# One combine moved behind a gate and up product, and a small projection split around a branch, in the expert layers of a two-block transformer kernel

## The chip, the cores and the metric

The kernel runs on one NeuronCore of a Trainium2 chip. The core has a matrix engine (PE in the profile, with its weight loads as PEld), a vector engine (DVE), a scalar engine (ACT), a general engine (POOL) and a sync engine (SP), whose queue here issues nearly all weight transfers. The engines run side by side, each through its own list of instructions in order, and wait for one another by semaphores. The metric is the device time of one execution in microseconds (us). Three executions of the kernel before took 853.91, 855.52 and 860.98 us.

## The reference, cut to what matters

The whole is an attention block with a dense feed-forward part, followed by two layers that each have attention, a mixture of 32 experts and a gated add of a per-layer input `p`. The change lies in the last two parts of each of the two layers:

```python
for i in range(DEPTH_2):                       # 2 layers
    ...
    h = h + hier_moe(rms_norm_2(h, ln_ffn[i]), ...)
    gate = jax.nn.sigmoid(rms_norm_2(h, ln_ple[i]) @ ple_w_gate[i])
    h = h + (gate * (p[i] @ ple_w_proj[i])).astype(h.dtype)

def hier_moe(xn, ...):                         # 256 tokens, 2 of 32 experts each
    hid = jax.nn.silu(jnp.einsum('td,edf->tef', xt, w_gate)) * jnp.einsum('td,edf->tef', xt, w_up)
    y = jnp.einsum('tef,efd->td', hid * cw[:, :, None], w_down)
```

`p[i]` is 256 x 256 and `ple_w_proj[i]` is 256 x 1024. The product of the two depends on neither the experts nor `h`, so it may stand anywhere ahead of the gated add.

## The kernel before, in words

`moe(l, router, rs)` computes the experts of layer `l` in eight passes `q` of four experts. The experts' weights are streamed once: each pass takes six panels of 1 MB from a stream `W`, four "gate_up" panels (one expert each, two transfers of 512 KB) and two "down" panels (two experts each). The stream's order is that of the generator `experts(l)`. A panel is issued on SP as soon as one of 21 buffers (the arena, tiles `a`) is free and the stream's limit allows it; the transfers use eight completion counters in rotation, so that an issue also waits for the transfer eight places before it.

A pass is this on PE. `gate_up` makes 64 small matmuls into one bank `gu` (line 1025). `hidden` turns the result on ACT and DVE into the hidden values `hd` (lines 1032 to 1034). `turn` transposes them on PE (`ht`, line 1038) and ACT copies the transpose (line 1039). `down` makes 16 matmuls (line 1045) into `y0` and `y1`, each of which ACT rounds (line 1049) and DVE takes the remainder of (line 1050). `combine` adds these to the accumulators `acc` of all tokens with eight matmuls (line 1056). The combine of a pass stands behind the *next* pass's `gate_up`, so PE has work while ACT and DVE make the hidden values. `gather` (line 993) and `slots` (lines 1009 to 1017, tile `ex`) prepare the rows and places of coming passes.

Pass 6 differs, since it is followed by `over.all`: a branch that reruns the chain of a pass for one expert that has more than 32 tokens (tiles `ov`, lines 1104 to 1147). In this input layer 0 takes the branch once and layer 1 does not. Ahead of pass 6's `gate_up` the kernel before makes the combine of pass 5 and the whole of `p @ ple_w_proj`: `ple_T` transposes `p` (four matmuls, tile `tps`, then ACT line 811 and DVE line 812), and `ple_proj` makes 24 matmuls in two halves of columns (tile `pj`, lines 543 to 545). Each half uses two pieces of the weight panel "ple_p", and each piece is first split by `split`: ACT (or POOL) casts it to a high part (line 538 or 536) and DVE (or POOL) subtracts for the low part (line 539). PE and SP keep the order in which the program is written; on ACT, DVE and POOL a scheduler orders the work when the program is built.

The `split` results, the gathered rows `xe` and the rounded `yd` share a ring of five buffers `s`; matmul results share eight PSUM banks, four of which the accumulators hold.

Of the kernel before, what the change touches and what calls it, by code (L numbers as in the profile page):

```python
# [203 lines left out]
class Stream:  # L204
# [24 lines left out]
    def next(self, key):  # L229
        if not self.ready:  # L230
            self.emit()
        k, name, views = self.ready.pop(0)
        assert k == key, (k, key)
        self.pump()
        return name, views
# [16 lines left out]
def block_kernel(ctx, tc, I, out):  # L252
# [14 lines left out]
    def bank(name="bank"):  # L267
        return psum.tile([128, 512], F32, tag="bank", name=name)
# [20 lines left out]
    def kpn(ap):  # L289
        return ap.rearrange("(k p) n -> p k n", p=128)  # L290
# [17 lines left out]

    def experts(l):
        for q in range(8):  # L310
            if q == 6:
                yield from panel("ple_p", kpn(I["ple_w_proj_2"][l]), 2)

            for i in range(4):
                ne, e, k0 = (1, 4 * q + i, 0) if q else (4, 0, 256 * i)

                def load(v, ne=ne, e=e, k0=k0):
                    v = v.rearrange("p (e a n) -> p e a n", e=ne, a=2)
                    for a, src in enumerate((I["moe_w_gate_2"], I["moe_w_up_2"])):
                        nc.sync.dma_start(v[:, :, a], src[l, e:e + ne].rearrange("e (p k) f -> p e (k f)", k=8)  # L320
                                          [:, :, k0:k0 + 1024 // ne])
                    return v

                yield "gate_up", 2048, load
            for e in range(4 * q, 4 * q + 4, 2):
                def load(v, e=e):
                    v = v.rearrange("p (e n) -> p e n", e=2)
                    nc.sync.dma_start(v, I["moe_w_down_2"][l, e:e + 2].rearrange("e p n -> p e n"))
                    return v

                yield "down", 2048, load
        for c in range(2):
            yield from panel("ple_g", kpn(I["ple_w_gate_2"][l])[:, :, c * 512:(c + 1) * 512], 4)
# [91 lines left out]
    def drain(g):  # L425
        for _ in g:
            pass
# [378 lines left out]
    def ple_T(pv_):  # L806
        pT = take("pT", [2, 2, S], F32R)
        b = bank("tps")
        transp2(lambda t, f: pv_[:, t, f * 128:(f + 1) * 128], 0, 2, b)
        hv, lv = [pT[:, i].rearrange("p a s -> p (a s)") for i in range(2)]  # L810
        A.copy(hv, b)
        V.tensor_tensor(lv, b, hv.bitcast(F32), OP.subtract)
        return [pT[:, 0], pT[:, 1]]

    def ple_proj(pT):
        pj = take("pj", [2, 1024])
        name, ws = W.next("ple_p")
        for c in range(2):
            ps = [bank("pj") for _ in range(2)]
            for k in range(2):  # L820
                acc_k(pT, k, ws[k][:, c * 512:(c + 1) * 512], ps, k == 0, k == 1)
                yield
            for t in range(2):
                A.copy(pj[:, t, c * 512:(c + 1) * 512], ps[t])
        W.drop(name)
        drop("pT")
        pjs.append(pj)
# [38 lines left out]
    def moe(l, router, rs):  # L866
# [185 lines left out]
        def combine(T, last):  # L1052
            for c in range(2):
                for hl in range(2):
                    for t in range(2):
                        mm(acc[t][c], T.d[:, t], T.yd[c][:, hl],  # L1056
                           start=False, stop=last and hl == 1)
                if last:
                    with tc.high_priority():
                        for t in range(2):  # L1060
                            (A.copy if t else V.tensor_copy)(h[:, t, c * 512:(c + 1) * 512], acc[t][c])

        class Overflow:
# [75 lines left out]
            def all(self, T, n):  # L1139
                R = Step(new_d(128), T)  # L1140
                self.pick(R.d)
                combine(T, False)
                R.yd = [R.ydt() for _ in range(2)]
                with tc.If(n > 0):
                    self.run(R)
                    with tc.If(n > 1):  # L1146
                        with tc.For_i(1, n, 1):
                            self.find()
                            self.load()
                            self.pick(R.d)  # L1150
                            self.run(R)
                drop("ovg", "ovd", "ovf")

        nrs = Rstd(f"rp{l}")
        prev = None
        for q in range(8):
            names, gu, dn = [], [], []
            if q == 6:
                combine(prev, False)
                prev = None  # L1160
                drain(ple_proj(ple_T(pv_)))
            for i in range(6):
                name, v = W.next("gate_up" if i < 4 else "down")
                names.append(name)
                (gu if i < 4 else dn).append(v)
            if q == 2:
                pv_ = ple_load(l)
            if q == 2:
                W.room(4)
            if q == 3:  # L1170
                over = Overflow()
            if q == 4:
                over.load()
                njob_r = nc.values_load(njob_i[0:1, 0:1], min_val=0, max_val=32)
            if q == 5:
                W.room(6 if l else 9)
            if q == 0:
                g = gather(d, Ts)
                next(g)
                acc_h(1, 1)  # L1180
            T = Ts.pop(0)
            ahead = not Ts and q < 7
            if ahead:
                d, Ts = steps()
            if q == 0:
                for i, _ in enumerate(gate_up(0, T, gu)):
                    if i == 1:
                        drain(g)
                        drain(slots(0, T))
                    W.drop(names.pop(0))  # L1190
            else:
                drain(gate_up(q, T, gu))
            if prev is not None:
                combine(prev, False)
            while len(names) > 2:
                W.drop(names.pop(0))
            fill = chain(gather(d, Ts) if ahead else (), slots(q + 1, Ts[0]) if Ts else ())
            later = rest(0)
            if q == 6:
                fill, later = later, fill  # L1200
            for _ in range(0 if q else 3):
                next(fill, None)
            turn(T)
            for _ in range(9 if q else 1):
                next(fill, None)
            down(T, dn)
            drain(fill)
            drain(later)
            for name in names:
                W.drop(name)  # L1210
            prev = T
            if q == 6:

                over.all(T, njob_r)
                drop("hr0", "hr1")
                prev = None
# [231 lines left out]
    for i, (k, c) in enumerate(jobs):  # L1448
# [4 lines left out]
        if i < 2:  # L1453
            k, c = jobs[i + 2]
# [638 lines left out]
```

## Time and profile before

| | |
|---|---|
| times of three executions | 853.91, 855.52, 860.98 us, median 855.52 |
| the profiled execution | 855.65 us, of which the span in the trace is 853.9 us |
| PE busy | 817.7 us, 96% of the span |
| DVE, ACT, POOL busy | 522.8, 445.1, 226.5 us |
| transfers | 201.71 MB, mean 236 GB/s |
| transfer rate in the later passes of each expert layer | 380 to 410 GB/s |
| mean granted PE clock | 0.994 of full speed |

The page gives busy times, the 40 slices of the span, and the chain of work that ended last. Two things help in reading it. A busy PE row includes matmuls that overlap one another, so the start times of successive groups tell more than their lengths. And a transfer's landing is told as the time from its issue; on SP, an issue that stands later than its neighbours' rhythm shows when an earlier transfer on the same counter landed.

### The profile page before, as it was taken

The numbers are of one execution on the slowest core, as the hardware profiler recorded it, in microseconds if no ns is written. First come the engines' busy times: TensorE is split into PE (matmuls) and PEld (weight loads), VectorE is DVE, ScalarE is ACT, GpSimd is POOL, SyncE is SP. The second block draws the span as 40 slices with busy tenths as digits, with TensorE's granted clock in tenths as the row PEclk, the third lists the DMA queues.
The fourth block names the chain that finished last, engine by engine and source line by source line (L and its number), as shares of the span: only waits on it lengthen the run. The fifth ranks groups of instructions, "written<-read, shape, count | busy, mean of one in ns | idle before, by whom it ended". The sixth has DMA issues, their size and how long they took to land. (4 is left out here: it accounts for less than half of the span.)

```text
span 853.9 us, 15690 instructions
## 1 busy us (share of the span) xinstructions
PE 817.7 (96%) x5660; PEld 639.4 (75%) x5660; DVE 522.8 (61%) x1520; ACT 445.1 (52%) x1085; POOL 226.5 (27%) x293
## 2 busy tenths in 40 slices
PE   8998999999999999999999999988999899999887
PEld 6897878999999988687667666765778577667556
DVE  5778766755455567678875725332888857353354
ACT  5675865644444456457865233332777843333353
POOL 2224542223222222423553400000324434000011
PEclk9999999999999999999999999999999999999999
DMA  9991429655565544173305689999964437899961
GB/s 319 385 376 54 155 74 399 238 178 192 198 197 178 171 152 151 64 244 124 125 1 188 264 333 406 406 409 385 370 221 127 195 106 247 304 405 406 409 245 50
DMA packets 85714, 201.71 MB, mean 236 GB/s; under 512 B 5840, under 2 KB 27776, under 8 KB 85632
## 3 DMA queue, kind: packets, MB, share of 16 engines
q1 hardware_dynamic: 83568, 198.36, 64.1%
q10 hardware_dynamic: 2064, 2.29, 0.9%
q8 instruction: 47, 0.77, 0.4%
q14 instruction: 35, 0.29, 0.1%
HBM read 199.57 MB, written 1.06 MB: 235 GB/s over the span
## 5 line engine op out<-in xcount | busy, mean ns | idle before, releaser
L539 DVE TENSOR_TENSOR s<-a,s 128x512 fp32r<-128x512 f32 (+3 forms) x281 | 189.6, 685 | 118.2 <-ACT s L538 85.7
L538 ACT CAST s<-a 128x512 fp32r<-128x512 f32 (+3 forms) x294 | 172.4, 600 | 161.5 <-PE pj L545 69.8
L543 PE MATMUL pj<-s,a 128*128 128x512 f32 (+3 forms) x456 | 176.0, 386 | 5.4 <-ACT a L520 3.9
L539 POOL TENSOR_TENSOR s<-a,s 128x512 fp32r<-128x512 f32 (+3 forms) x71 | 91.2, 1284 | 329.6 <-ACT s L538 287.7
L544 PE MATMUL pj<-s,a 128*128 128x512 f32 (+3 forms) x456 | 170.6, 374 | 5.2 <-DVE s L539 5.2
L545 PE MATMUL pj<-s,a 128*128 128x512 f32 (+3 forms) x456 | 169.8, 372 | 0.1
L543 PEld LDWEIGHTS pj<-s,a 128*128 128x128 f32 x456 | 86.1, 189 | 23.8 <-issue 5.9
L544 PEld LDWEIGHTS pj<-s,a 128*128 128x128 f32 x456 | 86.3, 189 | 20.0 <-DVE s L539 7.7
L545 PEld LDWEIGHTS pj<-s,a 128*128 128x128 f32 x456 | 86.2, 189 | 16.1 <-DVE a L521 1.5
L536 POOL TENSOR_SCALAR s<-a 128x512 fp32r<-128x512 f32 (+3 forms) x58 | 41.1, 709 | 196.3 <-PE pj L545 106.4
L1565 PE MATMUL f<-a,s 128*128 128x256 f32 x256 | 72.7, 284 | 0.0
L1567 PE MATMUL f<-a,s 128*128 128x256 f32 x256 | 72.4, 283 | 0.0
L1566 PE MATMUL f<-a,s 128*128 128x256 f32 x256 | 72.4, 283 | 0.0
L1025 PE MATMUL gu<-a,xe 128*32 128x256 f32 x1024 | 59.5, 380 | 1.7 <-PEq L1146 0.6
L1025 PEld LDWEIGHTS gu<-a,xe 128*32 128x32 f32 x1024 | 35.3, 110 | 26.7 <-issue 6.2
L543 PE MATMUL acc<-s,a 128*128 128x512 f32 x128 | 50.1, 391 | 0.0
L544 PE MATMUL acc<-s,a 128*128 128x512 f32 x128 | 49.9, 390 | 0.0
L545 PE MATMUL acc<-s,a 128*128 128x512 f32 x128 | 49.8, 389 | 0.0
L1565 PEld LDWEIGHTS f<-a,s 128*128 128x128 f32 x256 | 49.1, 192 | 0.2
L1566 PEld LDWEIGHTS f<-a,s 128*128 128x128 f32 x256 | 49.1, 192 | 0.2
L1567 PEld LDWEIGHTS f<-a,s 128*128 128x128 f32 x256 | 49.1, 192 | 0.0
L640 POOL TENSOR_SCALAR P<-P,nd 128x128 f32<-128x128 f32 x64 | 30.6, 490 | 49.2 <-DVE nd L635 19.8
(359 smaller groups left out, 1409.0 us busy)
## 6 DMA issues: line engine op xcount, KB each, us to landing
a<-in_moe_w_gate_dram SPq DMA_DIRECT2D x66, 512.0 KB, 8.0
a<-in_moe_w_up_dram SPq DMA_DIRECT2D x66, 512.0 KB, 8.6
a<-in_w_ff_dram SPq DMA_DIRECT2D x32, 1024.0 KB, 5.7
a<-in_moe_w_down_dram SPq DMA_DIRECT2D x32, 1024.0 KB, 10.6
a<-in_a_w_in_dram SPq DMA_DIRECT2D x10, 1024.0 KB, 5.1
a<-in_ple_w_gate_dram SPq DMA_DIRECT2D x8, 1024.0 KB, 16.1
a<-in_w_in_dram SPq DMA_DIRECT2D x6, 1024.0 KB, 14.0
a<-in_w_o_dram SPq DMA_DIRECT2D x4, 1024.0 KB, 13.2
```

The source lines that it names most:

```text
L536: G.tensor_scalar(hi, wv, 1.0, 0.0, OP.mult, OP.add)
L538: A.copy(hi, wv)
L539: (G if nsplit[0] % 5 == 2 else V).tensor_tensor(lo, wv, hi.bitcast(F32), OP.subtract)
L543: mm(ps, xh, hi, start=st, stop=False)
L544: mm(ps, xh, lo, start=False, stop=False)
L545: mm(ps, xl, hi, start=False, stop=sp)
L640: G.tensor_scalar(p[:, o0:o0 + n], p[:, o0:o0 + n], rc[:, t, i:i + 1], 1.0, OP.mult, OP.mult)
L1025: mm(b[32 * e:32 * e + 32, 0:256], T.xe[:, k, 32 * e:32 * e + 32], w, start=k == 0, stop=k == 7)
L1565: mm(o, hi[:, fs], xt[0][:, k], start=st, stop=False)
L1566: mm(o, hi[:, fs], xt[1][:, k], start=False, stop=False)
L1567: mm(o, lo[:, fs], xt[0][:, k], start=False, stop=sp)
```

## The change

Pass 6 no longer starts with the combine of pass 5 and the whole projection. Only the transposes of `p` stay there. The combine of pass 5 goes to the ordinary place, behind pass 6's `gate_up`. Behind pass 6's `down` and `slots` come the first half of the projection (12 matmuls), then the combine of pass 6 (taken out of `over.all`), then, in layer 1 only, the second half; in layer 0 the second half stands behind pass 7's `gate_up`. In the stream the panel "ple_p" moves behind pass 6's panels. In `ple_proj` the place of the second `yield` moves behind the copies of a half.

```diff
     def experts(l):
         for q in range(8):
-            if q == 6:
+            if q == 7:
                 yield from panel("ple_p", kpn(I["ple_w_proj_2"][l]), 2)
@@ ple_proj
                 acc_k(pT, k, ws[k][:, c * 512:(c + 1) * 512], ps, k == 0, k == 1)
-                yield
+                if not k:
+                    yield
             for t in range(2):
                 A.copy(pj[:, t, c * 512:(c + 1) * 512], ps[t])
+            yield
@@ Overflow.all
                 R = Step(new_d(128), T)
                 self.pick(R.d)
-                combine(T, False)
@@ moe, passes
             if q == 6:
-                combine(prev, False)
-                prev = None
-                drain(ple_proj(ple_T(pv_)))
+                pT = ple_T(pv_)
@@
             if prev is not None:
                 combine(prev, False)
+            if q == 7:
+                drain(ppj)
@@
             if q == 6:
+                ppj = ple_proj(pT)
+                for _ in range(2):
+                    next(ppj)
+                combine(T, False)
+
+                if l:
+                    drain(ppj)
 
                 over.all(T, njob_r)
```

On PE, in pass 6 of layer 0, before: the transpose of the hidden values, the down product into `y0` and `y1`, the places of pass 7 (`ex`), the combine, the branch.

```order
L1038 MATMUL ht<-ident_r,hd 128x128
L1045 MATMUL y_6212<-a_5880,hd 32x512 x2
L1045 MATMUL y_6212<-a_5882,hd 32x512 x2
L1045 MATMUL y_6220<-a_5880,hd 32x512 x2
L1045 MATMUL y_6220<-a_5882,hd 32x512 x2
L1009 MATMUL ex<-ident_r,d 128x128 x2
L1011 MATMUL ex<-cwr,d 128x10 x2
L1056 MATMUL acc<-yd,d 128x512 x8
L1144 COMPARE_AND_BRANCH
```

And in the change (the combine stands 12 matmuls further down, ahead of the branch):

```order
L1040 MATMUL ht<-ident_r,hd 128x128
L1047 MATMUL y_6165<-a_5799,hd 32x512 x2
L1047 MATMUL y_6165<-a_5880,hd 32x512 x2
L1047 MATMUL y_6173<-a_5799,hd 32x512 x2
L1047 MATMUL y_6173<-a_5880,hd 32x512 x2
L1011 MATMUL ex<-ident_r,d 128x128 x2
L1013 MATMUL ex<-cwr,d 128x10 x2
L543 MATMUL pj<-s,a_6102 128x512
L544 MATMUL pj<-s,a_6102 128x512
L545 MATMUL pj<-s,a_6102 128x512
```

What stood directly behind `ex` was the combine; now it is the first half of the projection, whose moving operand `s` is a split piece.

On ACT at the same place, before: the two roundings of `y0` and `y1`, the cast of the places `d`, the branch.

```order
L1039 COPY hd<-ht 128x128
L1049 CAST yd<-y_6212 128x512
L1049 CAST yd<-y_6220 128x512
L1013 CAST d<-ex 128x2x128
L1174 TENSOR_LOAD stage
L1144 COMPARE_AND_BRANCH
```

And in the change:

```order
L1041 COPY hd<-ht 128x128
L1051 CAST yd<-y_6165 128x512
L1051 CAST yd<-y_6173 128x512
L1015 CAST d<-ex 128x2x128
L538 CAST s<-a_5882 128x512 x2
L825 COPY a_6193<-pj 128x512 x2
L1173 TENSOR_LOAD stage
L1145 COMPARE_AND_BRANCH
```

The two casts of `split` stand behind the cast of `d`, which waits for PE's `ex`; on DVE the two subtractions likewise stand behind the remainder of `y1` and the two small instructions on `ex`.

On SP in layer 0, where pass 6's last panels, the branch's own loads and pass 7's panels follow one another, before:

```order
L328 DMA a_5880<-in_moe_w_down_dram 128x2x1024
L328 DMA a_5882<-in_moe_w_down_dram 128x2x1024
L320 DMA a_5884<-in_moe_w_gate_dram 128x1024
L320 DMA a_5884<-in_moe_w_up_dram 128x1024
L320 DMA a_5887<-in_moe_w_gate_dram 128x1024
```

And in the change:

```order
L328 DMA a_5880<-in_moe_w_down_dram 128x2x1024
L299 DMA a_5882<-in_ple_w_proj_dram 128x2x1024
L320 DMA a_5884<-in_moe_w_gate_dram 128x1024
L320 DMA a_5884<-in_moe_w_up_dram 128x1024
L320 DMA a_5887<-in_moe_w_gate_dram 128x1024
```

The second of the two 1 MB places ahead of pass 7 now holds "ple_p", and the first holds pass 6's *second* down panel; pass 6's gate and up panels have each moved one panel forward, and pass 7's panels stand where they stood. Layer 1 shows the same.

## Rows read from the trace of the kernel before

**Rows 1.** Windows, both layers: stretch, length, busy per engine (instructions), PE clock, DMA share, GB/s.
```profile
550.00:560.00 10.00, 9.24 (x57) 6.07 (x56) 4.73 (x11) 6.19 (x14) 1.28 (x1) 1.00 1.03 410
...
795.00:805.00 10.00, 8.67 (x86) 5.83 (x85) 1.95 (x7) 2.72 (x5) 0.62 (x1) 1.00 1.03 409
```

**Rows 2.** Timeline, PE, layer 0 passes 5 to 7: start, length, work, [idle <-releaser].
```profile
553.87 2.36 PE L1056 MATMUL acc<-yd,d 128*128 128x512 f32 x8
556.07 0.60 PE L503 MATMUL tps<-ident_r,ple_p 128*128 128x128 f32 x4
557.42 0.49 PE L543 MATMUL pj<-s,a 128*128 128x512 f32 x1 [0.76 <-ACT a L811]
...
563.38 3.66 PE L1025 MATMUL gu<-a,xe 128*32 128x256 f32 x64
568.54 0.30 PE L1038 MATMUL ht<-ident_r,hd 128*128 128x128 f32 x1 [1.50 <-DVE hd L1034]
569.20 1.92 PE L1045 MATMUL y<-a,hd 128*32 128x512 f32 x16 [0.36 <-ACT hd L1039]
...
571.47 2.09 PE L1056 MATMUL acc<-yd,d 128*128 128x512 f32 x8
573.40 3.69 PE L993 MATMUL ov<-d,a 128*128 128x128 f32 x32
...
587.76 3.99 PE L1025 MATMUL gu<-a,xe 128*32 128x256 f32 x64 [0.65 <-PEq L1146]
...
593.67 1.92 PE L1045 MATMUL y<-a,hd 128*32 128x512 f32 x16 [0.35 <-ACT hd L1039]
```

**Rows 3.** Timelines of ACT and DVE: a split, and pass 6's cast of its places.
```profile
559.38 0.62 ACT L538 CAST s<-a 128x512 fp32r<-128x512 f32 x1 [2.02 <-PE pj L545]
...
571.76 0.38 ACT L1013 CAST d<-ex 128x256 fp32r<-128x256 f32 x1
...
560.04 0.69 DVE L539 TENSOR_TENSOR s<-a,s 128x512 fp32r<-128x512 f32 x1 [1.94 <-ACT s L538]
```

**Rows 4.** Timeline of SP's queue, layer 0: issues.
```profile
540.53 0.42 SPq L320 DMA_DIRECT2D a<-in_moe_w_up_dram  x1
...
550.56 1.66 SPq L328 DMA_DIRECT2D a<-in_moe_w_down_dram  x2
...
562.06 0.33 SPq L320 DMA_DIRECT2D a<-in_moe_w_gate_dram  x1
564.57 0.33 SPq L320 DMA_DIRECT2D a<-in_moe_w_up_dram  x1
```

**Rows 5.** DMA issues, window of the issue at 540.53: size, us to landing.
```profile
a<-in_moe_w_up_dram SPq DMA_DIRECT2D x1, 512.0 KB, 12.5
```

**Rows 6.** Timeline, PE, layer 1 passes 5 to 7.
```profile
790.41 2.35 PE L1056 MATMUL acc<-yd,d 128*128 128x512 f32 x8
...
805.10 0.30 PE L1038 MATMUL ht<-ident_r,hd 128*128 128x128 f32 x1 [1.43 <-DVE hd L1034]
...
812.13 3.99 PE L1025 MATMUL gu<-a,xe 128*32 128x256 f32 x64 [0.41 <-DMA a<-in_moe_w_down_dram]
```

**Rows 7.** Timeline of SP's queue, layer 1: the last two issues of pass 7's gate and up.
```profile
797.91 0.33 SPq L320 DMA_DIRECT2D a<-in_moe_w_gate_dram  x1
800.42 0.33 SPq L320 DMA_DIRECT2D a<-in_moe_w_up_dram  x1
```

**Rows 8.** DMA issues, window of the issue at 800.42: size, us to landing.
```profile
a<-in_moe_w_up_dram SPq DMA_DIRECT2D x1, 512.0 KB, 11.8
```

**Rows 9.** Windows of 1 us at the two falls of PE's clock (columns as rows 1).
```profile
71.00:72.00 1.00, 0.00 (x0) 0.00 (x0) 1.00 (x2) 0.00 (x0) 1.00 (x2) 1.00 0.00 0
...
73.00:74.00 1.00, 1.00 (x4) 0.81 (x3) 1.00 (x1) 0.00 (x0) 1.00 (x1) 0.50 0.00 0
...
804.00:805.00 1.00, 0.00 (x0) 0.00 (x0) 0.86 (x4) 0.10 (x1) 0.00 (x0) 1.00 1.00 401
...
807.00:808.00 1.00, 1.00 (x8) 0.00 (x0) 0.44 (x1) 0.53 (x1) 0.00 (x0) 0.50 1.04 414
```

## The prediction

> **What bounds the kernel now.** I read the page first: the profiled execution took 855.65 us, its span is 853.9, so 1.75 lie outside; its time is 0.13 above the median of the runs shown, so what I work out against it holds for the median too. PE is busy 96% of the span, but that includes overlapping matmuls. So I went to the windows next: in both expert layers' late passes the DMA engines are full (share 1.03, 409 to 410 GB/s, [rows 1]), so two things are close to being the bound there, PE's order of work and the arrival of weights. The timeline of PE shows which of them ends last.
>
> In layer 0 it is PE. Between pass 5's combine (553.87) and pass 7's down product (593.67) PE never waits for weights; its gaps are 0.76 us (the projection waits for ACT's cast of the transposed input), 1.50 (pass 6's transpose waits for the hidden values, with nothing else to do), 0.36, 0.65 behind the branch, and, in pass 7, a gap of the same kind as the 1.50 and another 0.35 [rows 2]. In layer 1 it is the weights: pass 7's gate and up starts at 812.13 and waited for a transfer [rows 6]. The last of its panels was issued at 800.42 and took 11.8 us [rows 7, 8], which is 812.22. So in layer 1 PE's gaps of that stretch (1.43 in pass 6, [rows 6]) cost nothing today: without them PE would only have waited longer.
>
> **The change in layer 0, step by step.** I lay the new order on the old durations, starting at 553.87, where the transposes now stand.
>
> Transposes 0.60 (to 554.47). Then gate and up of pass 6: 3.66, the difference between its start and the end of its row [rows 2] (to 558.13). Its weights are there: the transfers ahead of the fourth panel's last are now the 4 MB that stood ahead of and in the third panel before, and that one was issued at 540.53 and took 12.5 us [rows 4, 5]: 553.03. Combine of pass 5: 573.40 - 571.47 = 1.93 [rows 2], to 560.06; it covers the hidden values, which took 1.50 beyond the product. So the 1.50 goes, and the 0.76 too: ACT's cast of the transposed input now has the whole gate and up beside it, and would cost its 0.76 again without that. Transpose to down product 0.66 (568.54 to 569.20): the down product may start at 560.72.
>
> Here the weights come in. The second down panel of pass 6 now stands in the first of two 1 MB places that were issued from 550.56 on. When did what stood there land? The issue eight places behind it, on the same counter, came at 562.06, late against the rhythm; the next at 564.57 [rows 4]. So these two places landed at about 562.06 and 564.57. Before, the down product came at 569.20 and neither mattered. Now four of the 16 matmuls run (0.48), PE waits 0.86 until 562.06, and the other twelve take 1.44: end 563.50.
>
> Next the first half of the projection, whose split pieces are late. ACT's cast of the places ends at 571.76 + 0.38 = 572.14, which is 1.02 behind the end of the down product (569.20 + 1.92); the split's cast stands behind it (0.62), then DVE's subtraction (0.69) [rows 3]. So the first matmul comes at +1.64, the second at +2.33, and the "ple_p" panel, landed at 564.57, is just in time (563.50 + 1.02 = 564.52). The 24 matmuls took 563.38 - 557.42 = 5.96, a half 2.98, a single one 0.25; eleven more after +2.33 end at +5.06, 568.56. What waits behind it is the combine of pass 6 (nothing to wait for any more, 1.93): 570.49. The branch starts there instead of at 573.40: **2.91 us gained**, of which 2.98 is only the second half, moved on.
>
> The branch itself and its 0.65 are unchanged; pass 7's gate and up would start at 584.85, and its weights, which stand in their old places, were issued up to 564.57 and need some 12 us. Then the second half: 2.98 on PE. Its split pieces are made while gate and up runs (3.66 against two times 0.62 + 0.69), so they cost nothing; without this cover each would cost 1.31. It hides the gap for pass 7's hidden values. Before, from gate and up to down product took 593.67 - 587.76 = 5.91. Now 3.66 + 2.98 = 6.64 to the transpose, and ACT must first make two copies of the half's results (0.62 each by the nearest row, the second from 6.64 on) before it copies the transpose (0.3): 7.5. That gives back **1.6**. Layer 0: 2.91 - 1.6 = **1.3 us gained**. Nothing between there and layer 1 waits for weights on PE, so it is passed on.
>
> Bounds of the unknown: the arrival of the down panel costs 0.86; if it is early, nothing (gain 2.2). The split's lateness, 2.33, is between 0 (gain 3.6) and 2.33 + 0.69, should the scheduler's order on DVE cost another subtraction (gain 0.6). I take the middle because the order of both engines is written down and its rows are the same instructions.
>
> [...]
>
> **The change in layer 1.** The same steps from 790.41: down product possible at 797.26, weights at 797.91 [rows 7], end 799.35; first half to 804.41, combine to 806.34, second half to 809.32. PE is ready 2.4 us sooner than before, but pass 7's weights stand behind the same bytes of a full queue, 812.22. So gain 0, and PE now idles 2.8 us there instead of 0.41.
>
> [...]
>
> **Sum.** 855.65 - 1.3 + 0 + 1.2 = 855.55, say **855.5 us**: no change that can be measured.
>
> **The rivals.** (1) The clock does not fall at pass 7 of layer 1. For it: gaps of 1.5 passed without a fall; against it: 2.8 is longer. 855.65 - 1.3 = 854.3. (2) The weights do not bind: they land sooner than the issue rhythm tells, in layer 0 (0.86 more) and in layer 1 (2.4 more). Against it the wait of 0.41 in the trace and a full queue. 855.65 - 1.3 - 0.9 - 2.4 = 851.1. (3) Slower: PE's clock falls already in pass 6 of layer 0, where PE now idles 0.86 and then 1.64 and about 0.45 within five microseconds, against 1.50 and 0.36 before. [...]
>
> **How the numbers follow.** My forecast 0.48, (1) 0.28, (2) 0.10, (3) 0.10, (4) 0.01, something not seen 0.03. The range reaches from near (2) to beyond (3), **851.5 to 858.0**; the runs of before lie 853.91 to 860.98, so it is also what their scatter asks for. 1% is 8.6 us, about what a measurement of this kernel can tell from no change; all cases named lie within it. Faster by over 1%: 0.02, within 1%: 0.95, slower by over 1%: 0.03.
>
> **What the changed profile would show.** Layer 0: pass 6's gate and up directly behind the transposes of `p`, and the combine between it and `ht` with no gap of 1.5. A short wait of the down product for a down panel. A gap of 1.2 to 1.7 before the first matmul of the projection, released by ACT's split, and a small one before the second, released by DVE's. The branch 2.9 sooner after pass 5. In pass 7 of layer 0 no gap before `ht`, but 1.6 more between gate and up and down product. Layer 1: a wait of 2 to 3 us for weights before pass 7's gate and up, and the clock at 0.5 within or shortly behind it. Now the two starts of pass 7's gate and up lie 812.13 - 587.76 = 224.37 us apart [rows 2, 6]; by my sum it becomes 226.0, since layer 0's moves by 2.9 and layer 1's by 1.3. Less than 225 would show that the weights are not what layer 1 waits for, and a projection without a wait ahead of it in pass 6 would show that the split is not late.

## The result and the profile after

The changed kernel took 853.7 us (median of 15, 850.39 to 854.83), the kernel before 860.4 (median of 15, 853.73 to 866.53): a ratio of 0.9931, 95% interval 0.9905 to 0.9956. The profiled executions differ by much less: 855.65 before, 854.15 after, spans 853.9 and 852.3. So there are two questions: where the 1.5 us of the profiles went, and why the medians are 6.7 apart.

**The profiles.** Cut at the first matmul of the down products ("y") of passes 5 and 7, the two spans are:

| stretch (us) | before | after | difference |
|---|---|---|---|
| start to pass 5 of layer 0 | 552.01 | 551.41 | -0.60 |
| layer 0, pass 5 to pass 7 | 41.66 | 40.84 | -0.82 |
| to pass 5 of layer 1 | 194.89 | 196.05 | +1.16 |
| layer 1, pass 5 to pass 7 | 29.48 | 28.15 | -1.33 |
| to the end | 35.8 | 35.8 | 0 |

The first and third lines are no work of the change: before's clock fall at 73 [rows 9] is missing after, and after has one near 669 that before has not. These two windows of the profile after show both (stretch, length, busy of PE, PEld, DVE, ACT, POOL with instructions, PE clock, DMA share, GB/s):

```profile
73.00:74.00 1.00, 0.91 (x4) 0.78 (x5) 0.96 (x3) 0.00 (x0) 1.00 (x2) 1.00 0.00 0
...
671.00:672.00 1.00, 1.00 (x7) 0.60 (x4) 0.39 (x3) 0.16 (x3) 0.32 (x1) 0.50 1.02 422
```

Without these two lines the change is worth 2.15 us in this pair. PE's timeline of layer 0 after answers to [rows 2]:

```profile
553.26 0.66 PE L503 MATMUL tps<-ident_r,ple_p 128*128 128x128 f32 x4
553.85 3.66 PE L1027 MATMUL gu<-a,xe 128*32 128x256 f32 x64
557.44 2.12 PE L1058 MATMUL acc<-yd,d 128*128 128x512 f32 x8
559.40 0.27 PE L1040 MATMUL ht<-ident_r,hd 128*128 128x128 f32 x1
560.02 1.05 PE L1047 MATMUL y<-a,hd 128*32 128x512 f32 x4 [0.35 <-ACT hd L1041]
561.61 1.91 PE L1047 MATMUL y<-a,hd 128*32 128x512 f32 x12 [0.54 <-DMA a<-in_moe_w_down_dram]
...
565.00 0.49 PE L543 MATMUL pj<-s,a 128*128 128x512 f32 x1 [0.99 <-ACT s L538]
565.73 0.50 PE L544 MATMUL pj<-s,a 128*128 128x512 f32 x1 [0.23 <-DVE s L539]
568.36 1.98 PE L1058 MATMUL acc<-yd,d 128*128 128x512 f32 x8
570.17 3.69 PE L995 MATMUL ov<-d,a 128*128 128x128 f32 x32
...
584.42 4.04 PE L1027 MATMUL gu<-a,xe 128*32 128x256 f32 x64 [0.55 <-PEq L1147]
588.38 0.50 PE L543 MATMUL pj<-s,a 128*128 128x512 f32 x1
591.24 0.27 PE L1040 MATMUL ht<-ident_r,hd 128*128 128x128 f32 x1
592.24 1.92 PE L1047 MATMUL y<-a,hd 128*32 128x512 f32 x16 [0.73 <-ACT hd L1041]
```

The 0.76 and the 1.50 of [rows 2] are gone; new are a wait for a down panel (0.54), two for the split (0.99 and 0.23), and 0.73 for ACT in pass 7. Layer 1 after, beside [rows 6]:

```profile
803.82 1.98 PE L1058 MATMUL acc<-yd,d 128*128 128x512 f32 x8
809.19 0.82 PE L1027 MATMUL gu<-a,xe 128*32 128x256 f32 x6 [0.68 <-ACT a L825]
810.92 3.61 PE L1027 MATMUL gu<-a,xe 128*32 128x256 f32 x58 [0.91 <-DMA a<-in_moe_w_up_dram]
...
816.45 1.92 PE L1047 MATMUL y<-a,hd 128*32 128x512 f32 x16 [0.35 <-ACT hd L1041]
```

The last gate and up panel of pass 7, the one of [rows 7, 8], was issued here at 799.62; the DMA issues of that window give its size and the us to its landing:

```profile
a<-in_moe_w_up_dram SPq DMA_DIRECT2D x1, 512.0 KB, 11.2
```

By this it landed at 810.82, where 812.22 was before.

### The profile page after: what moved, and what is told of

Same layout as the page of the kernel before. It is cut to its first block, busy times and chain, and to the rows that moved or that the text cites. A ratio compares the mean times of both kernels' runs of the same rounds, so it can differ in the third digit from the quotient of the medians.

```text
span 852.3 us, 15684 instructions
## 1 busy us (share of the span) xinstructions
PE 816.2 (96%) x5660; PEld 638.1 (75%) x5660; DVE 523.3 (61%) x1520; ACT 444.6 (52%) x1085; POOL 226.4 (27%) x293
```

## The experiments

They ran in three groups, each on one chip beside the kernel before. Group 1: the kernel before again, one layer, only the combine (kernel before beside them 857.76). Group 2: no branch, shorter jump, half late (859.45). Group 3: few weights, layer 0 without the branch, combine first, both (859.56). A table behind them has the stretches of all. A "long" execution is one of those that lie some 4 to 6 us above the rest, which for the kernel before means above 859.

### The kernel before, again

No edit.

> The kernel before, unchanged, run as a control beside itself. Fifteen executions of it lie between 853.73 and 866.53 us with a median of 860.40, its profiled one at 855.65; those of the changed kernel lie between 850.39 and 854.83. The two profiled executions differ by 1.5 us, the medians by 6.7. Theory A (clock): the long executions hold more stretches in which TensorE's clock is granted at half. One such stretch in the profiles lasts 3.41 us and lowers the mean granted clock of an execution by 0.002; the changed kernel's executions go from 850.4 at a mean of 0.998 to 854.7 at 0.992, about 1.3 us for each fall. By this theory the executions near 862 show a mean clock of 0.982 or less, those near 855 some 0.993, and the profile of a long one shows the falls. Theory B (transfers): the mean clock is the same in both groups (0.990 to 0.996) and the time is lost to weights that land later; a profile of a long execution shows PE waiting for DMA where the first profile has no such wait.

Measured: 860.43 (854.09 to 862.93, 12 runs). The mean clock of the executions tells part of it, not the whole: 0.998 goes with 854.1 to 854.6, 0.996 with 855.1 to 855.4, but 0.993 with 861.6 (twice) and 0.991 with 859.1 to 861.8. Those near 862 are not at 0.982, so theory A falls in the form given. The profile fell on a long execution (861.64). Up to pass 6's down product in layer 1 it lies 0.2 us or less from the first profile; all that it is longer arises from there to pass 7's down product (805.58 to 824.02, 18.44 us, where 12.28 stand in the first profile). PE's timeline there:

```profile
805.58 3.28 PE L1045 MATMUL y<-a,hd 128*32 128x512 f32 x16 [0.36 <-ACT hd L1039]
808.80 0.69 PE L1009 MATMUL ex<-ident_r,d 128*128 128x128 f32 x2
809.14 0.49 PE L1011 MATMUL ex<-cwr,d 128*128 128x10 f32 x2
809.49 2.10 PE L1056 MATMUL acc<-yd,d 128*128 128x512 f32 x8
816.99 5.12 PE L1025 MATMUL gu<-a,xe 128*32 128x256 f32 x64 [5.40 <-PEq L1144]
```

PE waits for no weights: it waits 5.40 us for its own sequencer, at line 1144, the branch around the experts that overflow. In layer 1 none overflows, so PE jumps. The branch stands in no list of busy time; its line's own view has it (duration in ns min/median/max, start). First the long execution, then the first profile of before:

```profile
L1144 PEldq COMPARE_BRANCH  x1: 6165/6165/6165, 810.3 to 810.3; - x1
```

```profile
L1144 PEldq COMPARE_BRANCH  x1: 1875/1875/1875, 809.8 to 809.8; - x1
```

In layer 0, where PE doesn't jump, the same branch took 0.09 us in both. What PE waits for is, by what follows, code. The page's DMA part lists a queue of instruction loads, q8: 47 loads, 0.77 MB, so 16 KB each; beside them the page has 11,320 instructions on PE and PEld, 241 for each load.

```profile
q8 instruction: 47, 0.77, 0.4%
```

One of them began to move at 813.88 in the long execution, 3.55 behind the start of the branch, and at 809.22 in the short one, 0.61 ahead of it. The DMA view of the long execution's window 813.8 to 815.2 has it, and that of the short one's 809.0 to 810.4:

```profile
q8 instruction: 1, 0.02, 5.5%
...
q8 instruction: 1, 0.02, 5.0%
```

From there to the end of the branch it is 2.62 and 2.49 us; in the six other profiles with this jump and full queues it is 2.46 to 2.61. So where the branch is long, its end follows the moment at which its load moves. The weights' transfers fill the queues meanwhile, as windows of the long execution show:

```profile
815.00:816.00 1.00, 0.00 (x0) 0.00 (x0) 0.00 (x0) 0.00 (x0) 0.00 (x0) 1.00 1.04 367
...
817.00:818.00 1.00, 1.00 (x10) 1.00 (x14) 0.00 (x0) 0.00 (x0) 0.00 (x0) 0.50 1.04 383
```

The second row shows what comes on top: behind 5.4 us of idleness PE's clock is at half, and gate and up took 5.12 where 3.99 stand in [rows 6]. Theory C is then: the long executions are those in which PE waits at this branch for code whose load moves late. The runs of groups 2 and 3 test it.

### The change in one layer only

```diff
-            if q == 7:
+            if q == (7 if l == 0 else 6):
                 yield from panel("ple_p", ...)
...
             if q == 6:
-                pT = ple_T(pv_)
+                if l == 0:
+                    pT = ple_T(pv_)
+                else:
+                    combine(prev, False)
+                    prev = None
+                    drain(ple_proj(ple_T(pv_)))
```

and so at the other places; for layer 1 alone the condition is l == 1.

> The change in the first expert layer alone (the second keeps the old order: combine of pass 5, then the whole projection, then gate and up of pass 6; its weights for the projection are queued where they were). If layer 0's two gaps of pass 6 bring on what makes the executions of the kernel before long (theory A: falls of the clock; one fall behind the 1.50 and 0.36 us gaps), the long executions are gone and the median is 855 or below. If layer 1's do, the long ones stay: median near 859. By the forecast's sum alone, without long executions, it is 855.65 - 1.3 = 854.3, and by the profile after 855.65 - 0.9 = 854.8.

> The change in the second expert layer alone (the first keeps the old order). If the long executions come from layer 0's pass 6, they stay: median near 859, mean clock low. If from layer 1's, they go: 854 or below. The forecast's sum gives layer 1 a gain of 0, or a loss of 1.2 with a fall of the clock; the profile after shows pass 7's down product 1.3 us sooner there beside layer 0's 0.9, so by that trace this run is 855.65 - 1.3 = 854.3.

Measured: layer 0 alone 856.75 (853.93 to 863.56; ratio 1.0002, 0.9973 to 1.0031), layer 1 alone 853.75 (852.09 to 857.35; ratio 0.9955, 0.9931 to 0.9979). With layer 1 alone none lies above 857.35; with layer 0 alone three lie above 860, so there some long ones stay; its median was expected near 859 if they did. What makes them is in layer 1, and the change there removes them. The profile of layer 0 alone doesn't show a long branch: its execution took 860.64 with a branch of 2.66 and a mean clock of 0.989, lower than in any other profile but the next kernel's, so falls of the clock lengthened it too.

### Only the combine moved

```diff
             if q == 6:
-                combine(prev, False)
-                prev = None
                 drain(ple_proj(ple_T(pv_)))
```

> Only pass 5's combine moves behind pass 6's gate and up in both layers; the projection of the layer's inputs stays whole ahead of gate and up, its weights are queued where they were, and pass 6's combine stays in the branch's code. The combine fills the wait for the hidden values (1.50 and 1.43 us), but the projection now stands directly behind its transposes and waits for their cast as before (0.76), with the combine no longer ahead of it to prepare its split. By the forecast's steps layer 0 gains 1.50 and gives nothing back in pass 7: 855.65 - 1.5 = 854.2 in an execution like the profiled one. If filling that wait is what takes the long executions away, its median is like the changed kernel's, 853 to 855; if the split of the projection (which fills pass 7's wait for the hidden values) does it, the long executions stay.

Measured: 876.5 (872.39 to 880.93, 6 runs; ratio 1.0227, 1.0182 to 1.0272), a miss by 22. The stretch of layer 0 took 51.52 instead of 41.66. PE's timeline, with those of the projection's 24 matmuls that waited:

```profile
555.27 0.50 PE L543 MATMUL pj<-s,a 128*128 128x512 f32 x1 [1.21 <-ACT s L538]
556.18 0.55 PE L544 MATMUL pj<-s,a 128*128 128x512 f32 x1 [0.41 <-DVE s L539]
...
559.14 0.79 PE L543 MATMUL pj<-s,a 128*128 128x512 f32 x1 [0.71 <-ACT s L538]
...
563.57 0.79 PE L543 MATMUL pj<-s,a 128*128 128x512 f32 x1 [1.19 <-ACT s L538]
564.91 0.80 PE L544 MATMUL pj<-s,a 128*128 128x512 f32 x1 [0.55 <-POOL s L539]
...
568.17 0.80 PE L543 MATMUL pj<-s,a 128*128 128x512 f32 x1 [0.76 <-ACT s L538]
```

The combine that stood ahead of the projection had covered its splits: before, ACT had cast three of the four by 556.88, ahead of the projection's first matmul at 557.42 [rows 2], and PE had no gap within it. Without it PE waits 4.83 in all (4.94 in layer 1). And in layer 0 the clock fell to half at 556.5, behind the 1.21 and the 0.41, and came back at 573.6; the matmuls stand 0.43 apart there, 0.23 in layer 1 where the clock stayed. The stretch lost 9.86 although the 0.76 and 1.50 of [rows 2] went, so 12.1 are to be found: 4.83 are these waits, 4.8 are 24 matmuls by 0.2, 1.1 is gate and up at half clock (4.74 beside 3.66), and 1.4 I did not follow. My expectation had priced the combine's place by what it newly covers and not by what it had covered.

### No branch in layer 1

```diff
                 R.yd = [R.ydt() for _ in range(2)]
-                with tc.If(n > 0):
-                    self.run(R)
-                    ...
+                if not l:
+                    with tc.If(n > 0):
+                        self.run(R)
+                        ...
```

for the kernel before and for the changed one alike.

> The kernel before without the branch for overflowing experts in the second layer: its body isn't there, and the compare and jump neither (part of the computation left out; for these inputs the second layer has no such expert, so nothing else is left out). In a long execution of the kernel before, PE's compare-and-branch of layer 1 took 6.17 us where a short one took 1.88, with PE idle 5.40 behind it, and a 16 KB load on the instruction queue moved 3.55 us after the branch began instead of 0.61 us ahead of it; PE went on 1.4 us after that load landed in both. Theory C: the time of the long executions is this wait for the code behind the branch, whose load stands beside a full queue of weights. Then without the branch there are no long executions: all between 853 and 857, median 854 to 855.5, since the weights still set 812. Theory A (falls of the clock in pass 6) and theory B (weights that land later): the branch is not the cause, the long executions at 858 to 863 stay, median 857 to 860.

> The changed kernel without the same branch in the second layer (the same part of the computation left out). Theory C: in the changed kernel PE meets the branch 4.3 us sooner (805.49 instead of 809.83) with the projection's second half still to run, and pass 7's weights come only at 810.9, so the wait for the code is covered even when it is 6 us long; without the branch nothing is gained: 852 to 854 median, beside 853.7 with it. The distance to the kernel before without the branch is then what the change is worth by itself, by the two profiles some 0.9 in layer 0 and 1.3 in layer 1: 1.5 to 2.5 us instead of the 6.7 of the medians. If the change does something else that makes the executions short, the distance stays 4 us or more.

Measured: before without the branch 854.52 (852.05 to 856.78), the long executions are gone, 4.9 below the kernel before beside it. Changed without it 851.64 (849.98 to 853.64, 7 runs; expected 852 to 854). That is 2.1 below the changed kernel, which ran in another group; at equal mean clock it is only 0.5 to 0.8 (0.993: 854.16 and 853.64; 0.997: 852.47 and 851.69, means), and the stretch of layer 1 is 0.35 shorter, so the branch costs the changed kernel less than the medians say. The distance of the two without branch is **2.9 us**, a little above the 1.5 to 2.5 forecast from the profiles. At equal mean clock it is 1.6 (0.997) and 2.2 (0.993): part of the 2.9 is that the seven executions of the changed kernel held fewer falls.

So of the 6.7 us some 2.9 are left without the branch, and the other 3.8 come and go with it. The split is rough, since the median of the kernel before depends on how many of its executions were long: it came to 857.76, 859.45, 859.56, 860.4 and 860.43. As the cause of the long executions the branch is shown; A and B fall.

Without the branch PE begins pass 7's gate and up directly behind the combine, with no wait for weights, 23.11 behind pass 5's down product (786.83) where [rows 6] have 23.57:

```profile
809.94 3.66 PE L1025 MATMUL gu<-a,xe 128*32 128x256 f32 x64
```


### A shorter jump

```diff
+                else:
+                    with tc.If(n > 0):
+                        with tc.For_i(0, n, 1):
+                            self.run(R)
+                            self.find()
+                            self.load()
+                            self.pick(R.d)
```

for layer 1 of the kernel before, in place of a first body and a loop.

> The kernel before with the branch kept, but the code that it jumps over in the second layer halved: one body in a loop that starts at 0, in place of a first body and a loop from 1 (the same computation for any input). The jump is about half as long in PE's program. If the wait is for code that PE hasn't loaded because the jump leaves what was loaded ahead, a shorter jump may land in what is loaded: then the branch takes 0.2 to 0.4 us as the jumps of layer 0 do (0.36 and 0.19), and the median is 854 to 855.5 with no long executions. If any jump at this place has its load behind the weights, the long ones stay, median 857 to 860, with 1.9 to 6.2 us at the branch.

Measured: 856.43 (852.42 to 861.08; ratio 0.9973, 0.9943 to 1.0004). The branch's line in the profiled execution:

```profile
L1154 PEldq COMPARE_BRANCH  x1: 222/222/222, 809.8 to 809.8; - x1
```

but five of the twelve still lie at 859.5 to 861.1. The median lies between the two that were expected. In the profile the branch ends 1.46 us behind the last instruction load that began ahead of it (808.52), not 2.46 to 2.62 as with the full jump; by that it did not wait for this load. The short branch gained nothing in layer 1's stretch, 29.50 beside 29.48. Whether the shorter jump helps on the whole these runs don't settle: the interval of the ratio reaches over 1.

### The second half of the projection late in both layers

```diff
                 combine(T, False)
-
-                if l:
-                    drain(ppj)
```

> The changed kernel with the projection's second half behind pass 7's gate and up in both layers (the change does this in layer 0 only). Layer 1: PE meets the branch at about 802.8, 3 us sooner still, with nothing of the projection ahead of it; even a 6.2 us wait for the code ends at 809, before pass 7's weights at 810.9. Theory C: no long executions. The projection's second half (2.98) then stands between gate and up (to 814.5) and pass 7's transpose in place of a gap of 1.26, and ACT's two copies stand ahead of the transpose's, which in layer 0 gave back 1.9: median 853.7 + 1.9 = 855.5. If instead it is the half product queued ahead of the branch that keeps the executions short, long ones come back, median over 857.

Measured: 855.87 (852.27 to 859.04; ratio 0.996, 0.9933 to 0.9986). The median is near the 855.5 expected, but not for the reason given: in the profile layer 1's stretch is 3.7 longer than in the changed kernel (31.89), with a fall of the clock over gate and up, and layer 0's is 1.1 shorter. Three of the twelve lie at 858.5 to 859.0, at mean clocks of 0.990 to 0.992; no profile shows what they hold. The one taken is telling: a long branch, early.

```profile
L1145 PEldq COMPARE_BRANCH  x1: 5546/5546/5546, 799.7 to 799.7; - x1
```

```profile
805.52 0.84 PE L1027 MATMUL gu<-a,xe 128*32 128x256 f32 x6 [1.97 <-PEq L1145]
807.70 6.52 PE L1027 MATMUL gu<-a,xe 128*32 128x256 f32 x58 [1.34 <-DMA a<-in_moe_w_up_dram]
```

The first fence is the branch's line, the second PE's timeline: 5.55 us at the branch, of which PE sees 1.97, and then it waits 1.34 for weights anyway. So this order does not make the branch short; PE meets it while there is time. In the changed kernel the one profile has a branch of 1.75 at 805.49, done at 807.24 while PE was busy with the projection's second half.

### Few weights

```diff
-                def load(v, ne=ne, e=e, k0=k0):
+                def load(v, ne=ne, e=e, k0=k0, few=l == 1 and q >= 6):
+                    m = 128 if few else 1024 // ne
...
-                        nc.sync.dma_start(v[:, :, a], ...[:, :, k0:k0 + 1024 // ne])
+                        nc.sync.dma_start(v[:, :, a, 0:m], ...[:, :, k0:k0 + m])
```

the down panels likewise, in the kernel before.

> The kernel before, branch and all, but with 9 of the 12 MB of expert weights of passes 6 and 7 of the second layer not loaded (those passes read the loaded part again and again, so their products are not the reference's; PE's instructions are the same). The transfer queues run nearly empty by the time PE meets the branch. Theory C says that the code behind the branch waits there because its load stands among the weights: then the branch takes its short time, 1.9 us or less, in every execution; pass 7's gate and up starts some 2 us behind the branch, no executions longer than the rest by 4 to 6, range 852 to 856. If the wait is a thing of the jump itself (a load asked for late, whatever the queues carry), 4 to 6 us long ones stay in about half of the executions.

Measured: 856.09 (853.79 to 858.59; ratio 0.9969, 0.9943 to 0.9995), half of them above the 856 expected at most, but none above 859, where 17 of the 27 executions of the kernel before beside it lie. The branch's line, windows ahead of it (columns as in [rows 1]), the DMA view of 808.5 to 809.0, and pass 7's gate and up on PE:

```profile
L1148 PEldq COMPARE_BRANCH  x1: 439/439/439, 811.1 to 811.1; - x1
```

```profile
806.00:808.00 2.00, 1.64 (x13) 0.55 (x16) 0.00 (x0) 0.27 (x1) 0.00 (x0) 0.73 1.05 391
808.00:809.00 1.00, 1.00 (x8) 0.00 (x0) 0.34 (x1) 0.59 (x1) 0.00 (x0) 0.50 0.59 205
809.00:810.00 1.00, 1.00 (x7) 0.42 (x3) 0.36 (x1) 0.25 (x1) 0.00 (x0) 0.50 0.00 0
```

```profile
q8 instruction: 1, 0.02, 13.9%
```

```profile
812.84 3.99 PE L1028 MATMUL gu<-a,xe 128*32 128x256 f32 x64 [0.40 <-PEq L1148]
```

The transfers ran out at about 808.6, and in that moment, at 808.60, the instruction load moved, 2.5 us ahead of the branch. So it had been asked for by then at the latest, while PE was still in pass 6's down product. That fits full queues holding it back in the kernel before; one profile doesn't prove it. Three executions at 858.0 to 858.6 with a mean clock of 0.995 are about 2.5 above those at 0.994 and 0.996 (855.4 to 856.4); I don't know why.

The run shows something else. With three quarters of these weights not loaded, layer 1's stretch is 29.51, where the kernel before has 29.48, and gate and up starts 23.61 behind pass 5's down product, where [rows 6] have 23.57. So in the short execution of the kernel before the weights were not what layer 1 waited for. The gap of 0.40 or 0.41 ahead of gate and up stands in all three profiles of layer 1's old order with a branch of 1.88 or less, however soon the branch and the weights were done (with the shorter jump the branch had ended 1.42 ahead of the product, and the last panel, issued at 799.54, had landed 1.66 ahead of it); without a branch it is gone, and gate and up takes 3.66 instead of 3.99.

### Layer 0 alone, without the branch in layer 1

Both edits shown above, together.

> The change in the first layer alone, and no branch for overflowing experts in the second (that part of the computation left out), so that the time of the branch doesn't lie over the comparison. Against the kernel before without that branch (854.52 median, 852.05 to 856.78) this is what layer 0's part is worth. The forecast gave it 1.3: 853.2. The profiles of kernels with it show 40.84, 40.87, 39.61 and 39.72 us from pass 5's to pass 7's down product where all without it show 41.63 to 41.66, so 0.8 to 2.0: 852.5 to 853.7. If layer 0's gain is lost before the end (taken up by falls of the clock between the layers, as one of 6.8 us in the profile of layer 0 alone), it is 854 to 854.5.

Measured: 853.67 (849.93 to 855.9), 0.85 below the 854.52 of before without the branch, which ran in another group, with both ranges over 4 us wide. At equal clock the distance is larger (0.997: 850.9 and 851.7 beside 853.1 to 853.3), but this kernel has more executions at a low one. In its profile the stretch of layer 0 is 39.69, 1.95 shorter, and 2.1 are lost again between the layers, in a fall of 6.8 us.

### Combine ahead of the projection, and both

```diff
                 ppj = ple_proj(pT)
+                combine(T, False)
                 for _ in range(2):
                     next(ppj)
-                combine(T, False)
```

> The changed kernel with pass 6's combine ahead of the projection's first half instead of behind it, in both layers. In the changed kernel PE waits 0.99 us for ACT's and 0.23 for DVE's piece of the first split there, because ACT and DVE still round the down product; the combine (1.93) has all it needs and would cover that. Layer 0 bounds its stretch by PE: 1.2 us less, 853.7 - 1.2 = 852.5. In layer 1 nothing, since pass 7's weights end last (810.8 to 810.9). If the combine then waits itself for the rounding of the down product (its pieces come from the same two engines), the gain is 0.3 or less: 853.4 to 853.7.

> Pass 6's combine ahead of the projection's first half, as in the kernel named h1_combine_first, and in the second layer one body for overflowing experts in a loop from 0 in place of two (the same computation for any input). The changed kernel without the branch came to 851.64, so the branch still costs up to 2 us there. With a jump half as long (0.22 us in a profile where it was 1.88) most of these 2 come back: 852.5 - 1.5 = 851.0. If the jump's length doesn't matter once PE meets the branch early, it is as h1_combine_first, 852.5.

Measured: combine first 852.27 (849.67 to 856.09, 10 runs; ratio 0.994, 0.9913 to 0.9968); with the shorter jump as well 850.26 (849.4 to 851.84, 6 runs; ratio 0.9919, 0.9889 to 0.9949). Expected were 852.5 and 851.0. The wait for the split is gone from PE's timeline of layer 0 (combine first):

```profile
563.17 2.09 PE L1058 MATMUL acc<-yd,d 128*128 128x512 f32 x8
565.10 0.40 PE L543 MATMUL pj<-s,a 128*128 128x512 f32 x1
```

The stretch of layer 0 is 38.15 and 38.02, 1.5 below the 39.6 to 39.7 of the changed order without a wait for the panel. By the medians both are below the kernel before, with intervals clear of 1, and below the changed one, which took 853.7 in another group; with that one they didn't run side by side, and the intervals of the ratios overlap with the changed kernel's and with each other. In both profiles with the shorter jump the branch took 0.22 us.

| kernel (us) | layer 0, y5 to y7 | layer 1, y5 to y7 | branch of layer 1 | median |
|---|---|---|---|---|
| before | 41.66 | 29.48 | 1.88 | 860.4 |
| before, long execution | 41.63 | 35.64 | 6.17 | 860.43 |
| changed | 40.84 | 28.15 | 1.75 | 853.7 |
| layer 0 only | 40.87 | 31.04 | 2.66 | 856.75 |
| layer 1 only | 41.65 | 27.58 | 1.84 | 853.75 |
| only the combine | 51.52 | 38.98 | 6.36 | 876.5 |
| before, no branch | 41.64 | 28.72 | none | 854.52 |
| changed, no branch | 39.61 | 27.80 | none | 851.64 |
| shorter jump | 41.64 | 29.50 | 0.22 | 856.43 |
| half late in both | 39.72 | 31.89 | 5.55 | 855.87 |
| few weights | 41.65 | 29.51 | 0.44 | 856.09 |
| layer 0 only, no branch | 39.69 | 28.76 | none | 853.67 |
| combine first | 38.15 | 28.62 | 2.43 | 852.27 |
| combine first, shorter jump | 38.02 | 27.24 | 0.22 | 850.26 |

(y5 to y7 is from the first matmul of pass 5's down product to that of pass 7's. Stretches and branch are of the one profiled execution and hold the clock falls that it had; the branch is the length of its record on PE, of which PE's idle time is only a part.)

## Why the prediction was right, and where it was not

The forecast of 855.5 (851.5 to 858.0) held the 853.7 and the "no change by over 1%". It did so with one step wrong, one thing not seen, and some luck.

**Layer 0, the order.** Each event forecast came: gate and up behind the transposes, the combine covering the hidden values, a wait for the down panel, a late split. The projection's matmuls that wait for ACT and for DVE came 1.48 and 2.21 behind the end of the down product (561.61 + 1.91 = 563.52; forecast 1.64 and 2.33). From the end of pass 5's down product to the branch it gained 2.62 (19.53 before, 570.17 - 553.26 = 16.91 after; forecast 2.91), and 1.91 went back between gate and up and the down product of pass 7 (7.82 against 5.91; forecast 1.6). Net 0.8 in this profile, forecast 1.3. The term that varies is the panel: in five of the six other profiles with layer 0's new order it comes earlier (first to last matmul of the down product 1.70 to 1.87 instead of 2.91, where 1.33 is without a wait), and the three of them that keep the change's order gain 1.9 to 2.0, near the bound of 2.2 that the text gave for it.

**Layer 1, the weights.** "Pass 7's weights stand behind the same bytes of a full queue, 812.22. So gain 0" is the step that failed: it took the weights for what bound layer 1. The stretch gained 1.33 in the profiles. Before, it was PE's own order, with the jump at its end, that bound it. The combine stood there until 811.71:

```profile
809.06 2.65 PE L1056 MATMUL acc<-yd,d 128*128 128x512 f32 x8
```

The branch ended at 809.83 + 1.88 = 811.71 too, and gate and up began 0.42 behind that. With three quarters of the weights not loaded, or with a branch of 0.22, it began no sooner (23.61 and 23.60 behind pass 5's down product, 23.57 here). So the reading under the step was wrong: [rows 6] put the 0.41 to DMA, but the gap is there without these weights and gone without the branch. In the long execution, where the weights had long been there, gate and up began 0.49 behind the branch (816.50, 816.99). The change makes PE's order shorter, and then the weights do bind: PE waits 0.91 for them after. That is the case of rival (2) in layer 1, which allowed 2.4 there.

They also came sooner than 812.22, at 810.82: 0.27 is the layer's own earlier start, 0.53 an earlier issue (799.62), 0.6 a shorter way (11.2 for 11.8). In the eleven other profiles that load this panel whole, it took 10.2, so the 11.8 that the forecast used was itself uncommon. The sign that the forecast named for this case, less than 225 between the two starts of pass 7's gate and up, came out at 809.19 - 584.42 = 224.77, though a fall of the clock between the layers lengthened it.

**The clock in layer 1.** Rival (1), no fall, is what the profiled execution shows: 854.3 forecast, 854.15 measured. PE idled 0.68 and 0.91 there, not 2.8 in one, and the clock was 1.00 in both microseconds. So no run shows the 1.2 that the sum takes for a fall of the clock there: in the changed kernel's profile none came, and where one lay over pass 7's gate and up, that took 5.12 for 3.99 (the long execution of before) or its last 58 matmuls 5.30 (combine first) and 6.52 (half late in both) for 3.61. Falls did come behind idleness elsewhere: in the first profile of before near 807 behind 1.43 and 0.36 ([rows 9], 0.50), while behind layer 0's 1.50 and 0.36 the clock stayed at 1.00; in the long execution of before behind 5.4 us, and with the combine alone behind 1.21 and 0.41. Gaps of one size don't settle it: with the combine first the clock fell at 806.5 behind 0.68 and 1.48, and with the shorter jump as well it did not behind 0.68 and 1.57.

**The sum.** In layer 1 both misses go the same way: 1.33 gained where 0 was forecast, and a fall of 1.2 that didn't come. They make the profiled execution 2.5 faster than forecast. Layer 0's smaller gain takes 0.5 of that back and the falls outside the passes (1.16 less 0.60) 0.6; so 854.15 stands beside 855.55.

**What was not seen** is the branch. More than half of the executions of before (65 of 113 lie above 859) are longer than the rest by some 4 to 6 us, which by the runs without the branch are lost there, and the trace that I read happened to be of a short one. That the forecast still held is luck: it was added up from a short execution and has no term for the branch, and the change happens to take the long ones away. From the median of the kernel before, 860.4, the same steps would have given 860.3, beyond the range. The scatter of the runs shown, 853.91 to 860.98, was in front of me; I used it to widen the range and did not ask what it was.

## What to carry to other kernels

A range of times far wider than the trace explains is a finding in itself: profile a slow execution before working out what a change is worth. Look at the branches' own lines on every engine that jumps, since the lists of busy time leave them out, and let the engine meet a jump while it still has work under way: here a branch of 5.55 us, met at 799.7, cost PE 1.97, and one of 6.17, met at 810.3, cost it 5.40. Before moving an instruction, ask what it covers where it stands, as well as what it would cover where it goes.

## What the runs showed of the hardware

A branch that jumps around code that isn't taken stood in PE's record for 1.75 to 6.36 us where the weights fill the transfer queues, for 0.44 where they had run out, and for 0.22 in both profiles where the jump was half as long. In the eight profiles with the full jump and full queues it ends 2.46 to 2.62 us after a 16 KB instruction load begins to move. When that load moves differs by more than 4 us between two executions of one kernel. Why, I can't say: no run looked at what stands ahead of it in its queue. Part of the record is covered by matmuls still under way: PE idled 0.41 for the 1.88, 5.40 for the 6.17. In layer 1's old order it idled 0.40 or 0.41 behind branches of 0.22 and 0.44 all the same, and its next product took 3.99 instead of 3.66; without the branch layer 1's stretch was 0.76 shorter (28.72 for 29.48).

Executions of one kernel differ in how many falls of the clock they hold, and each 0.002 of the mean clock goes with some 1.1 us (before without the branch: 852.05 at 1.000, 853.1 to 853.3 at 0.997, 854.2 to 854.7 at 0.995, 855.5 to 856.1 at 0.993). A fall between the layers, begun between 660 and 671 us, stands in four of the seven profiles with layer 0's new order and in one of the seven without it. Whether the new order brings it on, or chance, stays open; it would be why layer 0's 0.8 to 2.0 us show as only 0.85 in the medians.
